# Stick-breaking scans and products in pieces of 512 keys, key blocks taken from the highest down

## The chip, the core and the metric

The kernel runs on one core of one Trainium2 chip. The metric is the device time of one execution in microseconds (us). Five engines work from queues of their own and in the order of these queues: PE (matrix products, with PEld for its weight loads), DVE (vector work), ACT (activation functions and copies), POOL (GpSimd, elementwise work here) and SP, which issues nearly all DMAs.

## What is computed

One decoder layer: RMSNorm, one input projection, 8 heads of forgetting attention (softmax with a decay), 8 heads of stick-breaking attention, output projection, RMSNorm, a gated MLP with a causal convolution, final norm. 1024 positions, model width 1024, head width 64, float32. The change lies in the stick-breaking heads:

```
z = einsum('bhqd,bhkd->bhqk', q, k) * scale          # 128 queries, all keys
mask = kpos < qpos
log_one_minus = where(mask, log_sigmoid(-z), 0)
after = reverse cumsum over keys of log_one_minus, the key itself left out
weights = where(mask, exp(log_sigmoid(z) + after), 0)
out = weights @ v
```

So the weight of key s is sigmoid(z[s]) times the product of (1 - sigmoid(z[j])) over the keys j that lie between s and the query. The kernel works with the product itself: a running product from the last key down to the first.

## The kernel before

All matrix work is in float32r with operands split into a high and a low part, so that most products are three matmuls (`mm3`, lines 159 to 161) or, with the low half of one side left out, two.

**Attention** runs over 16 heads, the forgetting heads first (`p < NFOX`), then the 8 stick-breaking heads. A head has 8 query blocks `i` of 128, of which block i sees n = (i + 1) * 128 keys. Blocks 2g and 2g + 1 form group g, and the groups are taken in the order 0, 1, 3, 2 (`ORDER`).

`score(p, hb, i, ws)` (line 449) handles one query block: PE writes scores into PSUM in chunks of up to 512 keys (lines 466 to 470), ACT writes sigmoid(-z) into a tile `qt` and sigmoid(z) into `w[i]` (lines 480, 481). Two `qt` tiles (`NQ`) take turns; in traces they have the name `fbt`. Then, for a stick-breaking head, DVE makes the running product over all n columns of `qt` in place, from the highest column down (`tensor_tensor_scan`, line 493), and POOL multiplies `w` with it, shifted by one column (line 494). In the text this POOL operation is "the product".

`trans(g, mm, ws, box)` (line 497) transposes the weights of both blocks of a group for keys 256 mm to 256 mm + 255 on PE into a PSUM tile `tp` of 128x512 (line 505; there are two such tiles), ACT copies it into the high half `ph` (line 513), and DVE subtracts for the low half `pl` (line 514). A `tp` tile is free once `pl` is done. The tile on the diagonal (mm = g) needs three transposes in place of four and has tiles of its own, `pth` and `ptl`, 384 wide; the full ones share two pairs `ph`, `pl`.

`pv(p, hb, g, mm, box)` (line 517) multiplies V with the tile: four matmuls of 256 columns, two with the high half (line 525) and two with the low half (line 526), all of them summed in the one PSUM tile `o`. After the last, DVE folds `o` into the output (lines 534, 535).

**What sets the order.** `attention_stream` (line 566) writes the work of attention as a list: the scores of both blocks of a group, then the transposes and V products of the group before it (`prev`), three transposes ahead of the first V product (`LAG`). So the transposes of group 1 come behind the scores of blocks 6 and 7, those of group 3 behind the scores of blocks 4 and 5, and those of group 2 behind the first two blocks of the next head. Between the pieces `fill_to` puts matmuls of other work (projections of later heads, later the output projection), by costs that are written into the list. From this program order a scheduler sets the queues of PE, DVE, ACT and POOL; SP's queue stays as written.

POOL has other work in its queue as well: splitting weights (`wh`, `wl`, lines 142, 143), the low half of the projected q and k (`hl`, line 237) and sums (`oacc`, line 554).

Of the kernel before, what the change touches and what calls it, by code (L numbers as in the profile page):

```python
# [13 lines left out]
ALU = mybir.AluOpType  # L14
# [5 lines left out]
T = 1024  # L20
# [3 lines left out]
NFOX = 4  # L24
# [44 lines left out]
def layer(ctx, tc, xT, wqk, wv0, wv, wout, wup, wdn, cols, fbias, yT):  # L69
# [379 lines left out]
    def score(p, hb, i, ws):  # L449
        fox = p < NFOX  # L450
        q, kh, kl, vt, fbt = heads[p, hb]
        n = (i + 1) * P
        w = pp.tile([P, T], F32, name="w")
        ws[i] = w
        m = None
        if not fox:
            if len(qi) < NQ:
                qi.append(fp.tile([P, T + 1], F32, name="fbt"))
                nc.gpsimd.memset(qi[-1][:, T:T + 1], 1.0)
            qt = qi[count[0] % NQ]  # L460
            count[0] += 1
        for c0, cn in CHUNKS[i]:
            s = ps_s.tile([P, 512], F32, name="s")
            qb = q[:, i * P:(i + 1) * P]
            diag = c0 <= i * P < c0 + cn
            nc.tensor.matmul(s[:, :cn], qb, kh[:, c0:c0 + cn], start=True, stop=False)
            nc.tensor.matmul(s[:, :cn], qb, kl[:, c0:c0 + cn], start=False, stop=not diag)
            if diag:
                o = i * P - c0
                nc.tensor.matmul(s[:, o:o + P], identb, mask_f if fox else mask_s,  # L470
                                 start=False, stop=True)
            un = min(cn, n - c0)
            if fox:
                m2 = small.tile([P, 1], F32, name="m")
                nc.vector.tensor_tensor_reduce(  # L475
                    out=w[:, c0:c0 + un], in0=s[:, :un], in1=fbt[:, c0:c0 + un], scale=-1.0,
                    scalar=3.0e38 if m is None else m, op0=ALU.add, op1=ALU.min, accum_out=m2)
                m = m2
            else:
                act(qt[:, T - n + c0:T - n + c0 + un], s[:, :un], AF.Sigmoid, scale=-1.0)  # L480
                act(w[:, c0:c0 + un], s[:, :un], AF.Sigmoid)

        if fox:
            l = small.tile([P, 1], F32, name="l")
            act(w[:, :n], w[:, :n], AF.Exp, scale=-1.0, bias=m, accum_out=l)  # L485

            def rest():
                nc.vector.reciprocal(l, l)  # L488
                nc.gpsimd.tensor_scalar(w[:, :n], w[:, :n], l, 1.0, ALU.mult, ALU.mult)  # L489
        else:  # L490
            def rest():
                rev = slice(T - 1, T - n - 1 if n < T else None, -1)
                nc.vector.tensor_tensor_scan(qt[:, rev], qt[:, rev], qt[:, rev], 1.0, ALU.mult, ALU.bypass)  # L493
                nc.gpsimd.tensor_tensor(w[:, :n], w[:, :n], qt[:, T - n + 1:T + 1], ALU.mult)  # L494
        defer(0, rest)

    def trans(g, mm, ws, box):
# [18 lines left out]

    def pv(p, hb, g, mm, box):
        vt = heads[p, hb][3]
        if mm == 0:
            box["o"] = ps_o.tile([P, 256], F32, name="o")  # L520
        o = box["o"]
        ph, pl = box[mm]
        for a, kb in enumerate((2 * mm + 1, 2 * mm)):
            sl = slice(a * 256, (a + 1) * 256)
            nc.tensor.matmul(o, vt[:, kb, :], ph[:, sl], start=(mm == 0 and a == 0), stop=False)  # L525
            nc.tensor.matmul(o, vt[:, kb, :], pl[:, sl], start=False, stop=(mm == g and a == 1))  # L526
        if mm == g:
            h0 = hb * 64
            r, r2 = slice(h0, h0 + 64), slice(64 - h0, 128 - h0)
            ot = heads["o", p]  # L530
# [35 lines left out]
    def attention_stream():  # L566
# [3 lines left out]
        for n, (p, hb) in enumerate(hs):  # L570
            ws = {}
            order = ORDER_LAST if n == len(hs) - 1 else ORDER
            for gi, g in enumerate(order):
# [5 lines left out]
                    yield cost, partial(score, p, hb, i, ws)  # L579
                yield from prev  # L580
                box = {}
                tr = [(TRC, partial(trans, g, mm, ws, box)) for mm in range(g + 1)]
                pvs = [(0.67 - TRC, partial(pv, p, hb, g, mm, box)) for mm in range(g + 1)]
                prev = tr[:LAG]
                for mm in range(g + 1):
                    prev.append(pvs[mm])
# [708 lines left out]
```

## Time and profile before

| | |
|---|---|
| Median of 3 runs | 1442.48 us (1440.78 to 1443.48) |
| Profiled execution: its own time | 1441.58 us |
| Profiled execution: span of the core | 1439.6 us |
| PE busy | 1317.6 us, 92% |
| DVE, POOL, ACT busy | 1116.7, 859.4, 620.8 us (78%, 60%, 43%) |
| Stick-breaking heads | about 345 to 645 us of the span |

The span is what the trace covers; the execution's own time is 2 us longer. An engine that waits for a semaphore is not busy, but one that has started an instruction and is held up inside it is: a long instruction in the trace may be a held one. Matmuls are pipelined and their durations overlap, so that four matmuls of 0.28 us that start 0.12 us apart take 0.6 us. In a timeline, a number in brackets behind a row is the time that the engine stood idle before it, with the instruction that ended the wait.

### The profile page before, as it was taken

Reading aid. Unit: us, or ns where it says so; the run is one execution under the profiler, and the core shown is the slowest. Engines: PE = TensorE matmul, PEld = TensorE weight load, DVE = VectorE, ACT = ScalarE, POOL = GpSimd, SP = SyncE. Lnnn points to the kernel's source line nnn. Section 1 sums busy time; section 2 is a strip of 40 time slices with the busy share of each in tenths; the row PEclk is TensorE's granted clock in tenths of the full one; section 3 lists DMA queues with packets and bytes.
Section 4 is the critical chain, followed back from the end, with each engine's and each line's share of the span. In section 5 each row is a group of like instructions: output and inputs, shape, how many; then the busy total and the mean of one; then the engine's idle time right before and its main releaser. Section 6 shows DMA issues by size and latency. Waiting matters only on the chain.

```text
span 1439.6 us, 19147 instructions
## 1 busy us (share of the span) xinstructions
PE 1317.6 (92%) x6640; PEld 1075.9 (75%) x6640; DVE 1116.7 (78%) x1588; ACT 620.8 (43%) x1128; POOL 859.4 (60%) x730
## 2 busy tenths in 40 slices
PE   7899999999898887889778899999999998999995
PEld 5878878877787765777556688888888865878785
DVE  6246555655676677786899999998888889899987
ACT  5134434444454554353443434443443354344334
POOL 7344454543747573455667788878878763454423
PEclk9999999999999999999889999999999998999997
DMA  5556555545444454547311233333322355554313
GB/s 179 183 161 187 152 154 163 147 147 135 149 121 124 119 159 143 179 147 270 125 44 59 84 106 110 110 110 110 110 97 95 96 176 204 180 171 132 126 36 117
DMA packets 97232, 194.89 MB, mean 135 GB/s; under 512 B 8680, under 2 KB 35688, under 8 KB 97136
## 3 DMA queue, kind: packets, MB, share of 16 engines
q1 hardware_dynamic: 96272, 193.04, 42.6%
q8 instruction: 52, 0.85, 0.3%
q10 hardware_dynamic: 864, 0.64, 0.1%
q14 instruction: 44, 0.36, 0.1%
HBM read 132.79 MB, written 60.85 MB: 135 GB/s over the span
## 4 chain that ended last, share of the span: by engine, by line
PE 50%; DMA 18%; DVE 16%; POOL 7%; issue 6%; SPq 2%; ACT 2%; DVEq 0%; POOLq 0%; ACTq 0%
PE u L161 8%; PE u L160 8%; PE u L159 8%; PE pj L159 5%; PE pj L161 5%; PE pj L160 5%; DMA q<-qkd 4%; DVE fbt L493 3%; DMA vd<-vs 3%; DMA wraw<-in_wqk_dram 2%; DMA wraw<-in_wv_dram 2%; PE tp L505 2%; DMA fbt<-nfd 2%; PE o L526 2%; PE o L525 1%
## 5 line engine op out<-in xcount | busy, mean ns | idle before, releaser
L143 POOL TENSOR_TENSOR wl<-wraw,wh 128x256 fp32r<-128x256 f32 (+2 forms) x134 | 125.3, 952 | 26.9 <-ACT wh L140 21.3
L494 POOL TENSOR_TENSOR w<-w,fbt 128x128 f32<-128x128 f32 (+3 forms) x64 | 90.1, 1417 | 84.4 <-DVE fbt L493 59.9
L904 ACT CAST wh<-s 128x512 fp32r<-128x512 f32 (+1 forms) x136 | 79.8, 591 | 125.7 <-POOL s L879 71.0
L493 DVE TENSOR_TENSOR_SCAN fbt<-fbt 128x128 f32<-128x128 f32 (+3 forms) x64 | 103.5, 1624 | 25.9 <-ACT fbt L480 22.0
L142 POOL TENSOR_SCALAR wh<-wraw 128x256 fp32r<-128x256 f32 (+1 forms) x112 | 55.3, 509 | 108.8 <-DMA wraw<-in_wqk_dram 60.7
L878 POOL TENSOR_TENSOR s<-wraw 128x512 f32<-128x512 f32 (+1 forms) x34 | 55.8, 1641 | 96.0 <-DVE wl L906 53.5
L505 PE MATMUL tp<-ident,w 128*128 128x128 f32 x576 | 94.0, 281 | 19.5 <-DVE pl L514 9.5
L159 PE MATMUL pj<-xh,wh 128*128 128x512 f32 x224 | 103.1, 460 | 5.1 <-DVE yf L293 5.1
L906 POOL TENSOR_TENSOR wl<-wraw,wh 128x512 fp32r<-128x512 f32 x60 | 102.9, 1722 | 0.6 <-ACT wh L904 0.6
L505 PEld LDWEIGHTS tp<-ident,w 128*128 128x128 f32 x576 | 70.7, 144 | 39.1 <-DVE pl L514 12.6
L906 POOL TENSOR_TENSOR wl<-s,wh 128x512 fp32r<-128x512 f32 x48 | 88.5, 1845 | 13.8 <-ACT wh L904 13.4
L514 DVE TENSOR_TENSOR pl<-tp,ph 128x512 fp32r<-128x512 f32 x96 | 64.9, 685 | 40.9 <-ACT ph L513 40.5
L161 PE MATMUL pj<-xh,wl 128*128 128x512 f32 x224 | 91.9, 410 | 0.0
L160 PE MATMUL pj<-xl,wh 128*128 128x512 f32 x224 | 91.3, 407 | 0.0
L485 ACT ACTIVATE w<-w,m 128x128 f32<-128x128 f32 (+3 forms) x64 | 49.7, 776 | 91.1 <-DVE m L475 86.0
L1003 DVE SCALAR_TENSOR_TENSOR tg<-ua,col,tg 128x1023 f32<-128x1023 f32 (+1 forms) x44 | 88.1, 2002 | 0.0
L480 ACT ACTIVATE fbt<-s 128x512 f32<-128x512 f32 (+2 forms) x96 | 47.8, 498 | 83.8 <-PE s L470 39.2
L489 POOL TENSOR_SCALAR w<-w,l 128x128 f32<-128x128 f32 (+3 forms) x64 | 47.6, 748 | 59.9 <-DVE l L488 32.7
L904 ACT CAST wh<-wraw 128x512 fp32r<-128x512 f32 (+1 forms) x96 | 55.1, 589 | 63.1 <-DMA wraw<-in_wdn_dram 25.0
L1003 DVE SCALAR_TENSOR_TENSOR tv<-ub,col,tv 128x1023 f32<-128x1023 f32 (+1 forms) x44 | 76.0, 1727 | 5.7 <-ACT tv L1001 5.6
L513 ACT CAST ph<-tp 128x512 fp32r<-128x512 f32 x96 | 55.7, 590 | 53.1 <-PE o L525 33.4
L885 POOL TENSOR_TENSOR s<-wraw 128x512 f32<-128x512 f32 (+1 forms) x34 | 56.4, 1658 | 35.7 <-DVE wl L906 33.4
(409 smaller groups left out, 4569.4 us busy)
## 6 DMA issues: line engine op xcount, KB each, us to landing
wraw<-in_wup_dram SPq DMA_DIRECT2D x47, 512.0 KB, 3.6
qkd<-hl SPq DMA_DIRECT2D x32, 512.0 KB, 2.9
td<-tg SPq DMA_DIRECT2D x44, 256.0 KB, 2.3
vd<-vs SPq DMA_DIRECT2D x32, 256.0 KB, 4.5
q<-qkd SPq DMA_DIRECT2D x16, 512.0 KB
kh<-qkd SPq DMA_DIRECT2D x32, 256.0 KB, 16.6
kl<-qkd SPq DMA_DIRECT2D x32, 256.0 KB, 17.4
vt<-vd SPq DMA_DIRECT2D x16, 512.0 KB, 17.9
```

Source lines behind the costliest of these rows:

```text
L143: nc.gpsimd.tensor_tensor(self.lo[:, sl], self.raw[:, sl], f32(self.hi[:, sl]), ALU.subtract)
L159: nc.tensor.matmul(ps, ah, bh, start=start, stop=False)
L160: nc.tensor.matmul(ps, ah, bl, start=False, stop=False)
L161: nc.tensor.matmul(ps, al, bh, start=False, stop=stop)
L493: nc.vector.tensor_tensor_scan(qt[:, rev], qt[:, rev], qt[:, rev], 1.0, ALU.mult, ALU.bypass)
L494: nc.gpsimd.tensor_tensor(w[:, :n], w[:, :n], qt[:, T - n + 1:T + 1], ALU.mult)
L505: nc.tensor.transpose(tp[:, a * 256 + b * P:a * 256 + (b + 1) * P], ws[2 * g + b][:, kb * P:(kb + 1) * P], ident)
L514: nc.vector.tensor_tensor(pl[:, z:], tp[:, z:], f32(ph[:, z:]), ALU.subtract)
L885: nc.gpsimd.tensor_tensor(d["s3"], g[:, :w], v[:, :w], ALU.subtract)
L904: nc.scalar.copy(h[:, o:o + w], src)
L906: eng.tensor_tensor(l[:, o:o + w], src, f32(h[:, o:o + w]), ALU.subtract)
L1003: nc.vector.scalar_tensor_tensor(t[:, s:], us[:, :T - s], col[:, cw + tap:cw + tap + 1], t[:, s:], op0=ALU.mult, op1=ALU.add)
```

## The change

In stick-breaking heads the scan and the product are cut at key 512. For n up to 512 there is one of each as before. For n = 640, 768, 896 and 1024 the upper piece (128, 256, 384 or 512 columns) is scanned first, starting from 1.0, and then the lower piece of 512, starting from the last value of the upper one, which it reads from `qt`. Each piece has its own product; as the product is shifted by one column, the pieces there are n - 511 and 511 wide.

Transposes and V products of a stick-breaking head take the key pairs from mm = g down to 0 in place of 0 up to g, so that the diagonal tile comes first. The forgetting heads stay as they were.

```
-                rev = slice(T - 1, T - n - 1 if n < T else None, -1)
-                nc.vector.tensor_tensor_scan(qt[:, rev], qt[:, rev], qt[:, rev], 1.0, ALU.mult, ALU.bypass)
-                nc.gpsimd.tensor_tensor(w[:, :n], w[:, :n], qt[:, T - n + 1:T + 1], ALU.mult)
+                z = T - n
+                for a in range((n - 1) // 512 * 512, -1, -512):
+                    b = min(n, a + 512)
+                    rev = slice(z + b - 1, z + a - 1 if z + a else None, -1)
+                    nc.vector.tensor_tensor_scan(qt[:, rev], qt[:, rev], qt[:, rev],
+                                                 1.0 if b == n else qt[:, z + b:z + b + 1],
+                                                 ALU.mult, ALU.bypass)
+                    b = n if b == n else b - 1
+                    sl = slice(a - 1 if a else 0, b)
+                    nc.gpsimd.tensor_tensor(w[:, sl], w[:, sl], qt[:, z + sl.start + 1:z + sl.stop + 1],
+                                            ALU.mult)
...
-        if mm == 0:
+        begin, end = (0, g) if p < NFOX else (g, 0)
+        if mm == begin:
             box["o"] = ps_o.tile([P, 256], F32, name="o")
...
-            nc.tensor.matmul(o, vt[:, kb, :], ph[:, sl], start=(mm == 0 and a == 0), stop=False)
-            nc.tensor.matmul(o, vt[:, kb, :], pl[:, sl], start=False, stop=(mm == g and a == 1))
-        if mm == g:
+            nc.tensor.matmul(o, vt[:, kb, :], ph[:, sl], start=(mm == begin and a == 0), stop=False)
+            nc.tensor.matmul(o, vt[:, kb, :], pl[:, sl], start=False, stop=(mm == end and a == 1))
+        if mm == end:
...
-                tr = [(TRC, partial(trans, g, mm, ws, box)) for mm in range(g + 1)]
-                pvs = [(0.67 - TRC, partial(pv, p, hb, g, mm, box)) for mm in range(g + 1)]
+                keys = range(g + 1) if p < NFOX else range(g, -1, -1)
+                tr = [(TRC, partial(trans, g, mm, ws, box)) for mm in keys]
+                pvs = [(0.67 - TRC, partial(pv, p, hb, g, mm, box)) for mm in keys]
```

Line numbers of the changed kernel are a few higher: 493, 494 become 496 and 501, the low half 514 becomes 522, V products 525 and 526 become 534 and 535.

DVE's queue in the third stick-breaking head, from the scans of blocks 6 and 7 to the `pl` subtractions of group 3 (`fbt` is the scan tile, `full` belongs to a projection), before:

```order
L493 SCALAR_TENSOR_TENSOR fbt<-fbt 128x896
L493 SCALAR_TENSOR_TENSOR fbt<-fbt 128x1024
L514 TENSOR_TENSOR pl<-tp,ph 128x512
L514 TENSOR_TENSOR ptl_577<-tp,pth_576 128x384
L534 COPY tm<-o 64x256
L535 TENSOR_TENSOR ot<-o,tm 64x256
L493 SCALAR_TENSOR_TENSOR fbt<-fbt 128x640
L232 SCALAR_TENSOR_TENSOR full<-pj,rbc 128x512
L493 SCALAR_TENSOR_TENSOR fbt<-fbt 128x768
L514 TENSOR_TENSOR pl<-tp,ph 128x512 x3
L514 TENSOR_TENSOR ptl_575<-tp,pth_574 128x384
```

and now:

```order
L496 SCALAR_TENSOR_TENSOR fbt<-fbt 128x384
L496 SCALAR_TENSOR_TENSOR fbt<-fbt 128x512 x3
L522 TENSOR_TENSOR ptl_577<-tp,pth_576 128x384
L522 TENSOR_TENSOR pl<-tp,ph 128x512
L543 COPY tm<-o 64x256
L544 TENSOR_TENSOR ot<-o,tm 64x256
L496 SCALAR_TENSOR_TENSOR fbt<-fbt 128x128
L496 SCALAR_TENSOR_TENSOR fbt<-fbt 128x512
L232 SCALAR_TENSOR_TENSOR full<-pj,rbc 128x512
L496 SCALAR_TENSOR_TENSOR fbt<-fbt 128x256
L522 TENSOR_TENSOR ptl_575<-tp,pth_574 128x384
L496 SCALAR_TENSOR_TENSOR fbt<-fbt 128x512
```

At the first place four scans of 384, 512, 512 and 512 stand where there were two, still in one piece ahead of group 1's low halves (now `ptl`, then `pl`). At the second the diagonal `ptl` of group 3 stands ahead of the last scan piece (512), and the `pl` follow behind it; in six of the eight heads all four pieces are ahead of `ptl`.

PE's queue in the second stick-breaking head, the end of group 3's V products and the scores of the next head's first block (`pj` is filling work), before:

```order
L525 MATMUL o<-ph,vt 128x256
L526 MATMUL o<-pl,vt 128x256
L525 MATMUL o<-pth_574,vt 128x256
L526 MATMUL o<-ptl_575,vt 128x256
L525 MATMUL o<-pth_574,vt 128x256
L526 MATMUL o<-ptl_575,vt 128x256
L466 MATMUL s<-kh,q 128x256
L467 MATMUL s<-kl,q 128x256
L470 LDWEIGHTS identb
L470 MATMUL s<-mask_s,identb 128x128
```

and now:

```order
L534 MATMUL o<-ph,vt 128x256
L535 MATMUL o<-pl,vt 128x256
L466 MATMUL s<-kh,q 128x256
L534 MATMUL o<-ph,vt 128x256
L467 MATMUL s<-kl,q 128x256
L470 LDWEIGHTS identb
L470 MATMUL s<-mask_s,identb 128x128
L277 MATMUL pj<-wh,xh_236 128x256
L278 MATMUL pj<-wl,xh_236 128x256
L279 MATMUL pj<-wh,xl_244 128x256
L277 MATMUL pj<-wh,xh_237 128x256
L535 MATMUL o<-pl,vt 128x256
```

The diagonal tile (`pth`, `ptl`) was the last of the four V products and has gone to the front, so it is not in these rows any more. The last is now a full tile, and the next head's scores and filling matmuls stand between its first and second matmul.

## Rows read from the trace of the kernel before

**Rows 1.** The page, part 1: busy us (share of the span) xinstructions.
```profile
PE 1317.6 (92%) x6640; PEld 1075.9 (75%) x6640; DVE 1116.7 (78%) x1588; ACT 620.8 (43%) x1128; POOL 859.4 (60%) x730
```

**Rows 2.** Busy time by stretch, the stick-breaking heads; the columns in the first row.
```profile
core 0: us, PE busy (x) PEld busy (x) DVE busy (x) ACT busy (x) POOL busy (x), PEclk, DMA share, GB/s
...
345.00:645.00 300.00, 258.96 (x1520) 214.78 (x1519) 218.65 (x280) 148.48 (x314) 175.22 (x165) 0.95 0.47 141
...
```

**Rows 3.** Waits, 345 to 645: waiting <- awaited: us in total, times, longest.
```profile
POOL w L494 <- DVE fbt L493: 59.9, 21, 8.6
...
ACT ph L513 <- PE o L525: 21.3, 6, 8.6
ACT fbt L480 <- POOL w L494: 19.5, 8, 6.9
...
PE o L526 <- DVE pl L514: 10.8, 5, 3.2
...
PE tp L505 <- DVE pl L514: 6.1, 5, 2.0
...
PE tp L505 <- POOL w L494: 5.4, 4, 3.6
```

**Rows 4.** Timeline, second head, DVE then POOL: start, us, instruction [idle before <- releaser].
```profile
402.07 2.02 DVE L493 TENSOR_TENSOR_SCAN fbt<-fbt 128x896 f32<-128x896 f32 x1
405.02 3.17 DVE L493 TENSOR_TENSOR_SCAN fbt<-fbt 128x1024 f32<-128x1024 f32 x1 [0.92 <-ACT fbt L480]
...
408.75 0.68 DVE L514 TENSOR_TENSOR pl<-tp,ph 128x512 fp32r<-128x512 f32 x1
...
404.26 1.77 POOL L494 TENSOR_TENSOR w<-w,fbt 128x896 f32<-128x896 f32 x1 [3.11 <-DVE fbt L493]
408.36 2.00 POOL L494 TENSOR_TENSOR w<-w,fbt 128x1024 f32<-128x1024 f32 x1 [2.32 <-DVE fbt L493]
```

**Rows 5.** Timeline, third head, DVE then POOL, and POOL in the last head.
```profile
437.86 5.60 DVE L493 TENSOR_TENSOR_SCAN fbt<-fbt 128x896 f32<-128x896 f32 x2 [1.87 <-ACT fbt L480]
443.38 0.66 DVE L514 TENSOR_TENSOR pl<-tp,ph 128x512 fp32r<-128x512 f32 x1
...
438.31 3.00 POOL L237 TENSOR_TENSOR hl<-full,hl 128x512 fp32r<-128x512 f32 x1
441.27 5.71 POOL L494 TENSOR_TENSOR w<-w,fbt 128x896 f32<-128x896 f32 x2
...
618.16 3.00 POOL L143 TENSOR_TENSOR wl<-wraw,wh 128x512 fp32r<-128x512 f32 x1
```

**Rows 6.** Timeline of PE: four of its waits, and two matmuls in a row.
```profile
409.48 0.39 PE L526 MATMUL o<-pl,vt 128*128 128x256 f32 x1 [1.79 <-DVE pl L514]
409.70 0.28 PE L525 MATMUL o<-ph,vt 128*128 128x256 f32 x1
409.82 0.29 PE L526 MATMUL o<-pl,vt 128*128 128x256 f32 x1
...
444.10 0.39 PE L526 MATMUL o<-pl,vt 128*128 128x256 f32 x1 [2.20 <-DVE pl L514]
...
452.12 0.66 PE L505 MATMUL tp<-ident,w 128*128 128x128 f32 x4 [1.05 <-DVE pl L514]
...
480.10 0.39 PE L526 MATMUL o<-pl,vt 128*128 128x256 f32 x1 [3.21 <-DVE pl L514]
```

**Rows 7.** Timelines: scans of 512 and 1024 and a product of 512 alone.
```profile
574.66 1.22 DVE L493 TENSOR_TENSOR_SCAN fbt<-fbt 128x512 f32<-128x512 f32 x1
...
544.36 2.28 DVE L493 TENSOR_TENSOR_SCAN fbt<-fbt 128x1024 f32<-128x1024 f32 x1
...
400.06 1.09 POOL L494 TENSOR_TENSOR w<-w,fbt 128x512 f32<-128x512 f32 x1 [1.25 <-PE s L467]
```

**Rows 8.** Timelines of ACT and DVE: copy and subtraction of a full tile.
```profile
419.28 0.59 ACT L513 CAST ph<-tp 128x512 fp32r<-128x512 f32 x1 [1.53 <-PE o L525]
...
419.90 0.69 DVE L514 TENSOR_TENSOR pl<-tp,ph 128x512 fp32r<-128x512 f32 x1 [1.33 <-ACT ph L513]
```

## The prediction

> **What bounds the kernel now.** The first view is the page's busy table: PE is busy for 1317.6 of 1439.6 us, 92%, DVE for 78% and POOL for 60% [rows 1]. So the reader should look for the places where PE, in spite of that, stands still, and only those in which the changed lines run. The changed lines run in the second half of attention, from 345 to 645 us. The table by stretch gives PE 258.96 busy of 300 us there [rows 2], so about 41 us are idle. The table of waits of the same stretch says on what [rows 3]: V products wait 10.8 us for the low halves `pl` (DVE), transposes wait 6.1 us for the same `pl`, because the two PSUM tiles `tp` are freed by it, and transposes wait only 5.4 us for a finished product (POOL). The longest wait of the list, POOL 59.9 us for scans, is POOL being idle and costs nothing by itself.
>
> The timeline then shows why `pl` is late. At **place A**, V products of key pair group 1, `pl` stands on DVE behind the scans of query blocks 6 and 7: scan of 896 at 402.07, scan of 1024 from 405.02 for 3.17 us, `pl` at 408.75 [rows 4], and PE has waited 1.79 us [rows 6]. The same place costs 2.20 and 3.21 us in the next two heads [rows 6]. At **place B**, third transposes of group 3, `pl` stands behind the scans of blocks 4 and 5 (1.05 us in one head) [rows 6].
>
> What decides the length of these scans is POOL. A scan of 1024 takes 2.28 us when it is alone [rows 7], but 3.17 us where the product of 896 (404.26, 1.77 us) was already running: 406.03 is its end, and 406.03 plus 2.28 is 408.31, the scan's end within 0.1 us [rows 4]. So the scan did not share, it stood until the product was done. The reverse stands in rows 5: a POOL subtraction came at 438.31, inside a scan, and took 3.00 us, and two scans that need 2.02 and 2.28 us alone took 5.60 us together. The queue is scan (to 439.9), subtraction (to 441.3, so some 1.3 us), scan, and only then both products (5.71 us for 1.77 and 2.00 us of work) [rows 4, 5, 7]. A POOL operation that is waiting gets in at the boundary between two scans, and then DVE's turn comes. `pl` itself, which reads PSUM, runs at its usual length beside a product of 2.00 us [rows 4].
>
> The Trainium skill, page "SBUF — State Buffer", section "Who interferes with whom", states the same as a rule: a DVE instruction with two SBUF inputs and a GpSimd instruction that reads SBUF exclude one another for the whole instruction, and the one that issues first has it. By that rule a scan cut in two offers POOL one entry more in the middle, which speaks against this change; without it the products would simply run under the next scan. The trace agrees with the rule (3.17 us against 2.28 us alone).
>
> **The change, part by part.**
>
> Fixed costs. Blocks 4 to 7 of 8 heads get two scans and two products in place of one: 32 more of each. Two scans of 512 take 2 x 1.22, one of 1024 takes 2.28 us: 0.16 us per cut, 5.1 us of DVE in all. Two products of 512 take 2 x 1.09 against 2.00 us: 0.18 per cut, 5.8 us of POOL [rows 4, 7]. Neither engine is the bound, so this counts only at places A and B. The slope is (2.28 - 1.22)/512, 2.1 ns a column, and (2.00 - 1.09)/512, 1.8 ns, for products; so by estimate scans of 384, 256 and 128 take 0.96, 0.69 and 0.43 us, of 640 and 768 1.49 and 1.75 us, products of 384 and 128 0.87 and 0.41, of 640 1.32 us. The lower scan now starts from a value that the upper one wrote and waits for it; behind it on DVE stand the `pl` subtractions and the folds, for which PE waits.
>
> Place A. The order on DVE shows that nothing overtakes: where scans of 896 and 1024 stood ahead of `pl`, now 384, 512, 512, 512 do. Before, back to back: scan 2.02, product 1.77, scan 2.28, in all 6.07 us. After: POOL hears of the finished upper scan about 0.17 us later (404.09 to 404.26 [rows 4]), so the lower scan goes first; from then on they alternate: 0.96 + 1.22 + 0.87 + 1.22 + 1.09 + 1.22, 6.58 us. That is **+0.5 us**. Where another POOL operation was queued ahead of the products, as in rows 5, the line before was scan, subtraction, scan: 2.02 + 1.3 + 2.28, 5.6 us, with both products after `pl`. Now it is 0.96 + 1.3 + 1.22 + 0.87 + 1.22 + 1.09 + 1.22, 7.9 us: **+2.3 us**. I count three heads of that kind (the first, the third, the last; the last head's is the POOL subtraction at 618.16 [rows 5]) and five of the first: 9.4 us. PE's 10.8 us at this place are 5 waits [rows 3], so three heads (one of 2.3, two of 0.5) have no wait there that a delay would lengthen in full, and I take half of their 3.3: **7.8 us**. The bounds: 0.3 us for two fixed costs in the five heads that wait (1.6 us), and 2.3 us in all eight (18 us). A gain is excluded only as far as the alternation holds: if POOL never got in, the four scans would take 4.6 us and each place would gain about 1 us. I take the alternation, since rows 5 show it directly.
>
> Place B. The same arithmetic: 1.49 + 1.32 + 1.75 (scan and product of 640, scan of 768), 4.56 us before; 0.43 + 1.22 + 0.41 + 0.69 + 1.09 + 1.22, 5.06 us after: +0.5 us. Against it the first tile is now the diagonal one, whose `pl` is 384 wide instead of 512, a quarter of 0.69 us [rows 8] less, 0.15 us or so. In two heads (third and last) the new DVE order puts that diagonal `pl` ahead of the last scan piece, which helps the third transposes but delays the fourth, since the second `pl` comes after the piece: I put these at nothing. Six heads at 0.35 us: **2 us**, bounds -6.1 (all of the waits in rows 3 gone) and 4.
>
> Place C, new. In group 3 there are three full tiles and one diagonal one, and only two `ph`/`pl` pairs for the full ones. Before, the third full tile waited on the first V product, with a transpose and filling matmuls behind it (ACT waits such as 1.53 us in rows 8 hurt nobody). Now the diagonal one comes first and the last full tile waits on the V product two places ahead: copy 0.59, `pl` 0.69 [rows 8], about 1.4 us with the signals, against 4 matmuls at 0.12 us [rows 6] and the next head's scores that the order moved in between (0.5 to 1 us). Remainder 0.2 us in 8 heads: **1.6 us**, bounds 0 and 4.
>
> Gains of earlier products: PE waits for products only 5.4 us, 4 times [rows 3], nearly all of it where blocks of 256 to 512 keys are concerned, which are not cut. ACT waits 19.5 us for products that free the scan tile [rows 3], but with the alternation the last piece ends no earlier. Nothing.
>
> Sum: 7.8 + 2 + 1.6, 11.4 us on PE's path. I take off a quarter, as a wait made longer at A also lets POOL and DVE catch up before B: **+8 us**. The profiled execution took 1441.58 us (span 1439.6), so 1449.6; it lies 0.9 us under the median of 1442.48. On the median: 1450.5. I predict 1450.
>
> **The rivals.**
> Faster: the diagonal tiles come first and need only the upper piece, so PE's 6.1 us of waiting at B go and the products' 5.4 us shrink. For it: in two heads the diagonal `pl` does overtake a scan piece. Against it: in six it doesn't, and at B PE waits for DVE, not for POOL. It decides where POOL doesn't get in at the new boundary. Price -3 to -8 us: 1434 to 1439.5. Chance 0.13.
> No change: the alternation is real, but the waits at A are taken from slack, since scans often stand for ACT anyway (the scan of 1024 in rows 4 began 0.92 us after the one of 896 had ended). Then only fixed costs stay, 8 heads by 0.3 us: 1441 to 1445, in the middle 1444. Chance 0.20.
> Much slower: POOL gets in at every boundary of every head, so all eight heads pay 2.3 us at A, and PE's longer pauses cost clock (in this stretch the granted clock was 0.95 on the mean [rows 2]): 1456 to 1462. Chance 0.12.
>
> **How the numbers follow.** Forecast (1445.5 to 1456) 0.55, faster 0.13, no change 0.20, much slower 0.12. A measurement here tells about 0.2%, 2.9 us, from no change. So slower 0.67, same 0.20, faster 0.13. The range leaves out most of the faster case and the end of the much slower one: 1440 to 1459.
>
> **What would show it.** In the profile after: 96 scans with pieces of 512 that take 1.2 us alone and 2.1 to 2.3 us where a product was running; V products that wait for `pl` and `ptl` together more than the 10.8 us, by 5 to 10; transposes that wait for `pl` about as long as before; a new wait of the last V product of group 3 for ACT or DVE, 0.1 to 0.5 us each; PE busy unchanged in the sum, DVE and POOL busy up by at least 5 us each. The prediction is wrong if scans of 512 ahead of `pl` follow each other without a product between them, or if the waits at A shrink.

## The result, and the profile after

The changed kernel takes 1459.88 us (median of 4 runs, 1456.54 to 1462.12), the kernel before on the same chip 1441.63 us (1440.77 to 1443.48): ratio 1.0123, 95% interval 1.0099 to 1.0146. On two other chips the ratio is 1.0096 (1.0075 to 1.0118) and 1.0118 (1.0098 to 1.0138). So it is slower by 14 to 18 us. The forecast was 1450, with 1459 as the end of the range: the sign was right, and the 8 us too small for the 18 on that chip.

The profiled execution took 1460.76 us (span 1459.0). First the page's busy table, then the busy time of the stick-breaking stretch, which now ends at 664 us in place of 645 (columns as in [rows 2]):

```profile
PE 1324.8 (91%) x6640; PEld 1083.5 (74%) x6640; DVE 1126.2 (77%) x1620; ACT 622.9 (43%) x1128; POOL 875.6 (60%) x762
```

```profile
345.00:664.00 319.00, 266.46 (x1526) 222.31 (x1525) 231.32 (x313) 150.29 (x315) 193.46 (x197) 0.93 0.46 135
```

The span is 19.4 us longer, and about 19 us of that lie in this stretch. PE idles 319 - 266.46, 52.5 us, against 41.0 in [rows 2]: 11.5 us more. The other 7.5 us are PE being busy longer with the same work (266.46 against 258.96), while the mean granted clock of the stretch goes from 0.95 to 0.93. DVE has its 32 more instructions and 9.5 us more, POOL 32 more and 16.2 us more [rows 1].

The waits of the same stretch (waiting <- awaited: us in total, times, longest):

```profile
POOL w L501 <- DVE fbt L496: 53.0, 30, 4.6
...
PE o L535 <- DVE ptl L522: 19.4, 13, 3.7
...
PE tp L513 <- DVE ptl L522: 10.9, 7, 3.4
...
PE tp L513 <- POOL w L501: 6.6, 1, 6.6
```

The diagonal tile comes first, so PE now waits for its `ptl` where it waited for `pl`. Transposes wait 10.9 us for a DVE half where they waited 6.1, and for products 6.6 in one wait (in the first head) where there were 5.4 [rows 3]. DVE halves that the V products and transposes wait for, `pl` and `ptl` together: 20.0 us for V products (14.7 before, of that 3.9 for `ptl`) and 11.6 for transposes (6.1).

The timeline of the second head, DVE then POOL, and then the third head, shows the new boundary:

```profile
408.75 2.28 DVE L496 TENSOR_TENSOR_SCAN fbt<-fbt 128x384 f32<-128x384 f32 x2
411.70 3.43 DVE L496 TENSOR_TENSOR_SCAN fbt<-fbt 128x512 f32<-128x512 f32 x2 [0.67 <-ACT fbt L480]
...
415.70 0.55 DVE L522 TENSOR_TENSOR ptl<-tp,pth 128x384 fp32r<-128x384 f32 x1
...
409.88 2.85 POOL L501 TENSOR_TENSOR w<-w,fbt 128x385 f32<-128x385 f32 x2 [2.04 <-DVE fbt L496]
413.99 3.08 POOL L501 TENSOR_TENSOR w<-w,fbt 128x513 f32<-128x513 f32 x2 [1.25 <-DVE fbt L496]
```

```profile
445.07 7.18 DVE L496 TENSOR_TENSOR_SCAN fbt<-fbt 128x384 f32<-128x384 f32 x4 [1.87 <-ACT fbt L480]
452.17 0.53 DVE L522 TENSOR_TENSOR ptl<-tp,pth 128x384 fp32r<-128x384 f32 x1
...
445.53 1.93 POOL L237 TENSOR_TENSOR hl<-full,hl 128x512 fp32r<-128x512 f32 x1
447.43 6.76 POOL L501 TENSOR_TENSOR w<-w,fbt 128x385 f32<-128x385 f32 x4
```

In the third head two scans stood together before and took 5.60 us, while the subtraction `hl` was held for 3.00 us [rows 5]. Now four pieces, which need 0.96 + 3 x 1.22 = 4.6 us alone [rows 7 for the 512], take 7.18 us: DVE lost 2.6 us, because `hl` gets in after the first piece and a product piece after each of the next two. `hl` is the winner (1.93 us), the DVE half behind the scans the loser. PE's rows at this place (place A, heads two and three) and two of the longest at the third transposes (place B):

```profile
416.30 0.38 PE L535 MATMUL o<-ptl,vt 128*128 128x256 f32 x1 [1.92 <-DVE ptl L522]
...
452.75 0.55 PE L535 MATMUL o<-ptl,vt 128*128 128x256 f32 x1 [3.68 <-DVE ptl L522]
...
535.20 0.69 PE L513 MATMUL tp<-ident,w 128*128 128x128 f32 x2 [3.36 <-DVE ptl L522]
...
613.16 1.08 PE L513 MATMUL tp<-ident,w 128*128 128x128 f32 x4 [3.28 <-DVE ptl L522]
```

The second head's wait hardly grew (1.79 before), the third's grew by 1.5 (2.20 before) [rows 6].

### The profile page after: what moved, and what is told of

Same layout as the page of the kernel before. It is cut to its first block, busy times and chain, and to the rows that moved or that the text cites. A ratio compares the mean times of both kernels' runs of the same rounds, so it can differ in the third digit from the quotient of the medians.

```text
span 1459.0 us, 19213 instructions
## 1 busy us (share of the span) xinstructions
PE 1324.8 (91%) x6640; PEld 1083.5 (74%) x6640; DVE 1126.2 (77%) x1620; ACT 622.9 (43%) x1128; POOL 875.6 (60%) x762
## 4 chain that ended last, share of the span: by engine, by line
PE 52%; DMA 18%; DVE 15%; POOL 6%; issue 5%; SPq 2%; ACT 2%; DVEq 0%; ACTq 0%; POOLq 0%
PE u L160 9%; PE u L161 9%; PE u L159 9%; PE pj L159 5%; PE pj L161 5%; PE pj L160 5%; DMA q<-qkd 5%; DVE fbt L496 4%; DMA vd<-vs 3%; DMA kl<-qkd 2%; PE tp L513 2%; PE o L535 2%; DMA wraw<-in_wqk_dram 2%; PE o L534 2%; DMA fbt<-nfd 1%
## 5 line engine op out<-in xcount | busy, mean ns | idle before, releaser
L501 POOL TENSOR_TENSOR w<-w,fbt 128x128 f32<-128x128 f32 (+6 forms) x96 | 113.2, 1194 | 78.8 <-DVE fbt L496 53.0
L143 POOL TENSOR_TENSOR wl<-wraw,wh 128x256 fp32r<-128x256 f32 (+2 forms) x134 | 124.5, 946 | 23.4 <-ACT wh L140 19.4
L496 DVE TENSOR_TENSOR_SCAN fbt<-fbt 128x128 f32<-128x128 f32 (+3 forms) x96 | 112.6, 1180 | 27.2 <-ACT fbt L480 24.6
L513 PE MATMUL tp<-ident,w 128*128 128x128 f32 x576 | 94.3, 282 | 25.6 <-DVE ptl L522 10.9
L888 POOL TENSOR_TENSOR s<-wraw 128x512 f32<-128x512 f32 (+1 forms) x34 | 55.7, 1637 | 93.7 <-DVE wl L916 50.4
L522 DVE TENSOR_TENSOR pl<-tp,ph 128x512 fp32r<-128x512 f32 x96 | 65.2, 685 | 45.2 <-ACT ph L521 44.7
L916 POOL TENSOR_TENSOR wl<-s,wh 128x512 fp32r<-128x512 f32 x48 | 87.8, 1831 | 14.7 <-ACT wh L914 14.4
L480 ACT ACTIVATE fbt<-s 128x512 f32<-128x512 f32 (+3 forms) x96 | 47.6, 495 | 92.3 <-PE s L470 37.7
L277 PE MATMUL pj<-wh,xh 128*128 128x256 f32 (+1 forms) x256 | 78.6, 307 | 1.0 <-DVE yf L293 1.0
```

Source lines behind the costliest of these rows:

```text
L143: nc.gpsimd.tensor_tensor(self.lo[:, sl], self.raw[:, sl], f32(self.hi[:, sl]), ALU.subtract)
L277: nc.tensor.matmul(ps[:, :n], xh[k][:, sl], h, start=(k == 0), stop=False)
L501: nc.gpsimd.tensor_tensor(w[:, sl], w[:, sl], qt[:, z + sl.start + 1:z + sl.stop + 1], ALU.mult)
L513: nc.tensor.transpose(tp[:, a * 256 + b * P:a * 256 + (b + 1) * P], ws[2 * g + b][:, kb * P:(kb + 1) * P], ident)
L522: nc.vector.tensor_tensor(pl[:, z:], tp[:, z:], f32(ph[:, z:]), ALU.subtract)
L916: eng.tensor_tensor(l[:, o:o + w], src, f32(h[:, o:o + w]), ALU.subtract)
```

## The experiments

Each kernel below was timed beside the kernel before on the same chip, whose median there was 1445.9 to 1446.7 us. Microseconds in the table are the ratio's distance from 1 times 1446.

| Kernel | Ratio (95% interval) | us against before |
|---|---|---|
| scans and products cut, keys ascending, three chips | 1.0077 (1.0056 to 1.0097), 1.0076 (1.0053 to 1.0100), 1.0080 (1.0055 to 1.0104) | +11, +11, +12 |
| keys descending, nothing cut | 1.0001 (0.9989 to 1.0012) | 0 |
| scans cut, products whole, two chips | 1.0066 (1.0048 to 1.0084), 1.0061 (1.0038 to 1.0083) | +10, +9 |
| products cut, scans whole | 0.9995 (0.9983 to 1.0008) | -1 |
| before, second operand of the scans in PSUM | 0.9937 (0.9914 to 0.9961) | -9 |
| changed kernel, the same | 0.9940 (0.9920 to 0.9959) | -9 |
| cut, keys ascending, the same | 0.9947 (0.9930 to 0.9965) | -8 |
| scans in pieces of 256, products whole | 1.0077 (1.0050 to 1.0104) | +11 |
| scans of 896 and 1024 cut alone | 1.0032 (1.0016 to 1.0048) | +5 |
| scans of 640 and 768 cut alone | 1.0005 (0.9990 to 1.0020) | +1 |
| changed kernel, two chips | 1.0096 (1.0075 to 1.0118), 1.0118 (1.0098 to 1.0138) | +14, +17 |
| scans cut, products whole, keys descending | 1.0096 (1.0062 to 1.0130) | +14 |

### Which part of the change costs the time

My theory was that the price stands at the new scan boundary, where POOL gets in. The rivals were the order of the key blocks, and the fixed cost of more instructions. First each part alone. The cut alone is the kernel before with the new `rest()` of the diff, and the order alone is the changed kernel with the old `rest()`.

> The cut of scans and products alone, key blocks of transposes and V products ascending as before. Theory 1 (the price is the cut: at each new scan boundary a product piece of POOL gets in before the next scan, which makes the DVE operation that PE waits for later, at eight third-transpose places and eight V-product places, and PE's clock falls in the longer gaps): 1452 to 1459 us, PE waits at the third transposes like those of the changed kernel, about 3 us a head, and granted clock in the stick-breaking stretch about 0.93. Theory 2 (the price is the descending order, which makes the diagonal pair's transposes and its split first and so waits for the highest block's product): within 4 us of the kernel before, 1441 to 1446 us.

> The descending key order alone, scans and products whole. Theory 1: 1441 to 1446 us, of that about 2 us in the first head, where the diagonal's transpose now waits for the product of block 3. Theory 2: 1452 to 1460 us, with PE waits for the transposed diagonal pair in every head.

The cut alone costs 11 us, on three chips; the order alone costs nothing. So the cut is the cause of most of it. The expected place was wrong. With ascending keys, 345 to 655 us:

```profile
PE o L534 <- DVE pl L522: 17.1, 7, 3.8
...
PE tp L513 <- DVE pl L522: 5.4, 5, 2.7
```

The V products wait 17.1 us for `pl` (10.8 before) and the transposes 5.4 (6.1 before), so here nearly all of the rise in waits for DVE halves is at the V products.

Then the two halves of the cut:

```
-                nc.vector.tensor_tensor_scan(qt[:, rev], qt[:, rev], qt[:, rev], 1.0, ALU.mult, ALU.bypass)
+                for a in range((n - 1) // 512 * 512, -1, -512):
+                    b = min(n, a + 512)
+                    rev = slice(z + b - 1, z + a - 1 if z + a else None, -1)
+                    nc.vector.tensor_tensor_scan(qt[:, rev], qt[:, rev], qt[:, rev],
+                                                 1.0 if b == n else qt[:, z + b:z + b + 1],
+                                                 ALU.mult, ALU.bypass)
```

with the product as it was, and the other way round, with the scan as it was:

```
-                nc.gpsimd.tensor_tensor(w[:, :n], w[:, :n], qt[:, T - n + 1:T + 1], ALU.mult)
+                for a in range((n - 1) // 512 * 512, -1, -512):
+                    b = min(n, a + 512)
+                    b = n if b == n else b - 1
+                    sl = slice(a - 1 if a else 0, b)
+                    nc.gpsimd.tensor_tensor(w[:, sl], w[:, sl], qt[:, z + sl.start + 1:z + sl.stop + 1], ALU.mult)
```

> The scans cut in two, the products whole, key blocks ascending. Theory 1 (a boundary costs only where a piece of product is ready to get in at it; here a block's product waits for both of its scan pieces, so only the product of the block before can): 1443 to 1450 us, PE waits at the third transposes less than half of those of the changed kernel. Theory 3 (the fixed cost of 32 more scans and the slower clock that follows is enough): 1450 us or more, near the changed kernel's time.

> The products cut in two (upper piece first), the scans whole, key blocks ascending. Theory 1 (DVE's scan and POOL's product shut each other out for a whole instruction): at the V products of the second group the scan of 1024 waits for half a product (0.9 us) and not a whole one (1.8 us) and the split behind it comes 0.9 us earlier, in 8 heads 7 us at most, less what the product pieces lose to it later: 1435 to 1443 us. Theory 3 (fixed cost): 1444 to 1450 us, from 32 more POOL operations of about 0.15 us each and the splits they hold up.

The scan cut alone costs 9 us, the product cut alone nothing. By the times expected, both results spoke for theory 3, the fixed cost (1450 us or more for the scan cut, 1444 to 1450 for the product cut; measured 1456.97 and 1445.58), and only the runs below decide against it. I had expected the scan cut to be the cheaper of the two, on the idea that with whole products little is ready at the new boundary. The timeline of its third head, DVE then POOL, shows that something is:

```profile
448.93 7.24 DVE L496 TENSOR_TENSOR_SCAN fbt<-fbt 128x384 f32<-128x384 f32 x4 [1.87 <-ACT fbt L480]
456.09 0.66 DVE L519 TENSOR_TENSOR pl<-tp,ph 128x512 fp32r<-128x512 f32 x1
...
449.38 1.94 POOL L237 TENSOR_TENSOR hl<-full,hl 128x512 fp32r<-128x512 f32 x1
452.57 2.51 POOL L499 TENSOR_TENSOR w<-w,fbt 128x896 f32<-128x896 f32 x1 [1.25 <-DVE fbt L496]
```

The four pieces take 7.24 us again. Before, three POOL operations stood at this place and one of them got in, at the one boundary between the two scans [rows 5]. With three boundaries two of them do, `hl` and the whole product of 896 (held itself: 2.51 for 1.77 us of work [rows 4]). A boundary lets in whatever POOL has next; it needn't be a piece of the product.

The product cut was a miss of my theory: I expected up to 7 us of gain, since a scan would wait for half a product only. In its trace the V products' wait for `pl` does fall (10.8 to 8.2 us), but the transposes wait longer for products (5.4 to 8.3), and the time stays.

### Whether it is the exclusion

The scan has two SBUF inputs, both of them `qt`; the second is ignored by the bypass. If the exclusion hangs on that second input, it can be taken away without touching any order: let the ignored operand be a column of PSUM. A zero column beside the V products' accumulator serves.

```
+    oz = ps_o.tile([P, 512], F32, name="oz")
+    nc.vector.memset(oz[:, 256:257], 0.0)
+    zero = oz[:, 256:257]
...
-                nc.vector.tensor_tensor_scan(qt[:, rev], qt[:, rev], qt[:, rev], 1.0, ALU.mult, ALU.bypass)
+                nc.vector.tensor_tensor_scan(qt[:, rev], qt[:, rev], zero.to_broadcast([P, n]), 1.0, ALU.mult, ALU.bypass)
...
-            box["o"] = ps_o.tile([P, 256], F32, name="o")
+            box["o"] = oz[:, :256]
```

> The kernel before, whole scans and products, but the scan's second operand, which the bypass ignores, is one zero column of PSUM instead of the SBUF row itself. Theory 1 (a scan with two SBUF inputs and a POOL operation shut each other out for a whole instruction): with one SBUF input left the two run side by side, the pair of scans at the V products of the third head's second group takes 4.3 us instead of 5.6, that of the second head's 1024 block 2.3 instead of 3.2, and the splits behind them come as much earlier: 8 to 14 us below the kernel before. Theory 3 (fixed costs of instructions only, and no exclusion that depends on the operands): within 3 us of the kernel before, or slower by what a PSUM operand costs a scan.

> The changed kernel with the same zero column of PSUM as the scans' second operand. Theory 1: no POOL operation gets in at a boundary any more, what is left of the cut is its fixed cost of about 0.2 us per boundary: from 8 us below the kernel before to 4 us above it, at least 10 us below the changed kernel. Theory 3: 11 to 19 us above the kernel before, as the changed kernel.

> Scans and products cut in two, key blocks ascending, and the scans' second operand a zero column of PSUM. Without exclusion the cut has only its fixed cost, beside work that PE doesn't wait for: 6 to 11 us below the kernel before, as with whole scans. If finer pieces bring the splits and transposes forward once nothing gets in between, 12 us or more below it; if the fixed cost of 32 boundaries (0.2 us each on DVE) counts, 1 to 5 us below it.

All three run 8 to 9 us below the kernel before, and so beat both kernels: medians 1437.06, 1437.13 and 1438.68 us. With the second SBUF operand gone, the change as a whole costs nothing any more, neither the cut nor the order. So its 14 to 18 us need that operand, as the exclusion says. The third head of the kernel before with this one edit, DVE then POOL:

```profile
433.37 4.20 DVE L496 TENSOR_TENSOR_SCAN fbt<-fbt,oz 128x896 f32<-128x896 f32 x2 [1.05 <-ACT fbt L483]
437.49 0.67 DVE L517 TENSOR_TENSOR pl<-tp,ph 128x512 fp32r<-128x512 f32 x1
...
433.45 1.29 POOL L237 TENSOR_TENSOR hl<-full,hl 128x512 fp32r<-128x512 f32 x1
435.56 1.77 POOL L497 TENSOR_TENSOR w<-w,fbt 128x896 f32<-128x896 f32 x1 [0.81 <-DVE fbt L496]
```

The two scans take 4.20 us (5.60 before), and `hl` (1.29, before 3.00) and the product of 896 (1.77) run under them. Over all eight heads, the scans of 1024 (out<-in xcount | busy us, mean ns of one | idle before), first in the kernel before and then with the PSUM operand:

```profile
L493 DVE TENSOR_TENSOR_SCAN fbt<-fbt 128x1024 f32<-128x1024 f32 x8 | 23.5, 2941 | 1.0 <-ACT fbt L480 0.9
```

```profile
L496 DVE TENSOR_TENSOR_SCAN fbt<-fbt,oz 128x1024 f32<-128x1024 f32 x8 | 18.2, 2273 | 0.9 <-ACT fbt L483 0.8
```

The mean of 1024 is now 2.27 us, which is the scan alone [rows 7]. So what a scan took beyond that came with the second SBUF operand, beside POOL's work. PE's waits for `pl` follow, 345 to 645 us, but there is a new wait, the first row:

```profile
PE oz L528 <- DVE fbt L496: 4.3, 5, 1.6
...
PE tp L508 <- DVE pl L517: 1.9, 4, 0.9
...
PE oz L529 <- DVE pl L517: 0.8, 2, 0.7
```

Of 10.8 us of V products and 6.1 of transposes [rows 3], 0.8 and 1.9 are left. The new wait is a price of this edit: the zero column lies in the tile `oz` into which the V products are summed, and now their first matmul waits for scans that read it. With the cut it is longer, 6.4 us with keys descending and 9.2 ascending. No V product ran during any of these scans.

The Trainium skill, page "SBUF — State Buffer", section "Who interferes with whom", states that a DVE instruction with at most one SBUF input (outside its two-port modes) doesn't contend with GpSimd. These scans agree: 2.27 us on the mean beside running products.

The same operand in the changed kernel shows the fixed cost of the cut by itself. In its third head the four pieces take

```profile
433.55 4.69 DVE L499 TENSOR_TENSOR_SCAN fbt<-fbt,oz 128x384 f32<-128x384 f32 x4 [1.05 <-ACT fbt L483]
```

4.69 us against 4.20 for two whole scans: 0.25 us per cut on DVE, where the prediction had 0.16. The three kernels take the same time, so this cost stands beside other work. The third theory, fixed costs, was tested from the other side too, with pieces of 256 (two or three boundaries per block where there was one):

```
+                step = n if n <= 512 else 256
+                for a in range((n - 1) // step * step, -1, -step):
+                    b = min(n, a + step)
...
```

The product stays whole here.

> Scans of blocks above 512 keys in pieces of 256, products whole, key blocks ascending: three boundaries more for each 1024 or 896 block's two, ten per pair of blocks at two places where the version with pieces of 512 has four. Theory 3 (each boundary has its price on DVE, some 0.2 us): 10 us for pieces of 512 become 20 to 32 us above the kernel before. Theory 1 with exclusion alone (what a boundary costs is the POOL operation that it lets in, and there are no more whole products or other POOL operations ready than at pieces of 512): 10 to 16 us above it.

48 scans more than with pieces of 512, and 11 us against 9: no difference that these intervals can tell, where I expected 20 us or more of fixed costs alone. It fits the exclusion, if there are only so many POOL operations to let in; how many got in was not counted. (One reservation: in this kernel's third head one of the pieces stands behind `pl`, so the DVE order isn't quite the same.)

### Where in a head the price arises

The next two cut scans only at place A (blocks of 896 and 1024 keys) and only at place B (640 and 768), with products whole and keys ascending, by `step = 512 if n > 768 else n` and `step = 512 if 512 < n <= 768 else n`.

> Scans cut in two only for the blocks of 896 and 1024 keys, which stand ahead of the second group's V products (place A); products whole, key blocks ascending. By the prediction's sizes (7.8 of 11.4 us at A) this is 7 to 10 us above the kernel before, nearly all of what cutting every scan costs (10 us). By the rise of the waits in the changed kernel's trace, more at the third group's transposes (5.5 us) than at A (3.5 us), it is 3 to 5 us.

> Scans cut in two only for the blocks of 640 and 768 keys, which stand ahead of the third group's transposes (place B); products whole, key blocks ascending. By the prediction's sizes 1 to 3 us above the kernel before; by the rise of the waits in the changed kernel's trace 4 to 7 us.

Cut at A alone the kernel loses 5 us (2 to 7), less than the 7 to 10 by the prediction's sizes; at B alone 1 (-1 to 3), at both 9. The waits of the first, 345 to 650 us, tell more than the time:

```profile
PE o L532 <- DVE pl L520: 20.5, 8, 3.8
...
PE tp L511 <- POOL w L500: 5.5, 4, 3.7
...
PE tp L511 <- DVE pl L520: 3.2, 4, 1.5
```

V products wait 20.5 us for `pl`, 9.7 more than before. But PE's idle time of the stretch (305 - 259.77 = 45.2 us) is only 4.2 us longer, since the transposes wait 2.9 us less for `pl` and other waits shrink too. So it seems that what PE loses at A, DVE and POOL in part use to catch up. With every scan cut that is gone; the waits of the scan cut, 345 to 660 us:

```profile
PE o L531 <- DVE pl L519: 18.4, 8, 3.8
...
PE tp L510 <- POOL w L499: 6.8, 4, 5.1
PE tp L510 <- DVE pl L519: 6.5, 6, 2.8
```

V products wait 7.6 us more, and transposes at B 6.5, as much as before: the lengthened scans at B use up the lead. That 9 is more than 5 + 1 is at the edge of what the intervals resolve (3.9 us, give or take 3.7); the rows make the reason plausible, and I count it as shown only so far.

### What the order adds

With the cut, the descending order isn't free. One chip ran the changed kernel, the cut alone, and the scan cut with and without the descending order.

> The changed kernel itself, on the chip on which the other versions run. If the order of the key blocks costs only together with the cut, 15 to 19 us above the kernel before, against 11 for the cut alone; if the two do not add, 10 to 13 us above.

> The changed kernel beside the cut alone on one chip. If the descending order adds to the cut: 3 to 6 us above the cut alone, with waits at the seventh head's transposes of the third group that the ascending order doesn't have. If it adds nothing and the chips differed: within 2 us of the cut alone.

> The cut of scans and products with key blocks ascending once more, beside the others on their chip. If the descending order adds nothing to the cut, 11 to 17 us above the kernel before, as the changed kernel; if it adds some 3 to 6 us, 8 to 11 us above it.

> The cut of scans and products, key blocks ascending: 10 to 12 us above the kernel before, as on two other chips.

> Scans cut, products whole, key blocks ascending: 8 to 11 us above the kernel before, as on another chip.

> Scans cut, products whole, key blocks descending. If the order adds to any scan cut: 3 to 6 us above the same with ascending blocks. If it adds nothing: within 2 us of it.

With +14 for the changed kernel on one chip and +11 for the cut alone on another the question was open. On the common chip the changed kernel stands 5.5 us above the cut alone (1.0118 against 1.0080), the scan cut with descending keys 5.1 us above the one with ascending keys; taken together 5.3 us, give or take 3.6. In three profiles of the changed kernel the transposes wait 11.6 to 11.9 us for DVE halves, in three of the cut alone 5.4 to 5.9, while the V products wait about as long in both. One place can be read. The seventh head on the common chip, DVE then POOL, first the changed kernel, then the cut alone:

```profile
606.61 2.07 DVE L496 TENSOR_TENSOR_SCAN fbt<-fbt 128x256 f32<-128x256 f32 x2
608.60 2.56 DVE L663 TENSOR_TENSOR t<-xin,t 128x512 f32<-128x512 f32 x2
611.09 0.55 DVE L522 TENSOR_TENSOR ptl<-tp,pth 128x384 fp32r<-128x384 f32 x1
...
607.46 3.15 POOL L501 TENSOR_TENSOR w<-w,fbt 128x257 f32<-128x257 f32 x2 [3.84 <-DVE fbt L496]
```

```profile
607.80 0.68 DVE L522 TENSOR_TENSOR pl<-tp,ph 128x512 fp32r<-128x512 f32 x1
608.44 1.29 DVE L661 TENSOR_TENSOR t<-xin,t 128x512 f32<-128x512 f32 x2
```

and PE, two rows of the changed kernel, then one of the cut alone:

```profile
606.75 0.51 PE L159 MATMUL pj<-ogh,wh 128*128 128x512 f32 x1 [2.84 <-DVE t L662]
...
611.69 0.84 PE L513 MATMUL tp<-ident,w 128*128 128x128 f32 x4 [3.27 <-DVE ptl L522]
```

```profile
607.94 0.79 PE L159 MATMUL pj<-ogh,wh 128*128 128x512 f32 x1 [4.32 <-DVE t L660]
```

In the changed kernel the `ptl` for which the third transposes wait (3.27 us there) stands behind two additions of the output projection, which also have two SBUF inputs and are held by the products: 2.56 us for 1.29. With ascending keys, where `pl` stands ahead of them, the transposes don't wait here; the projection matmul before them waits 1.5 us longer instead, so the two waits together are 6.1 us against 4.3. The scan cut with whole products and descending keys has no such wait of the transposes either, at 6.3 us of transposes waiting for `ptl`. Its profiled execution, 1471.61 us, was the slowest of six (the others took 1452 to 1459), with PE busy for 1333.1 us, so its rows are a poor guide to its 5 us. The lengths of the heads, from one head's first score matmul to the next one's, point the same way in both pairs: the seventh takes 3.9 to 4.1 us longer than in the kernel before in three profiles of the changed kernel and -1.2 to 1.3 in three of the cut alone; with products whole it is 3.1 with keys descending, and 1.0 and -0.8 ascending. So the size of the order's share is measured, give or take 3.6, and its place only in part.

## Why the prediction was wrong, step by step

**Bound and mechanism: right.** That scans and POOL operations stand for each other, that POOL gets in at the new boundary, and that the halves behind the scans make PE wait, is what the timelines and the PSUM operand showed: without the second SBUF operand the change costs nothing. In the third head four pieces were worked out at 7.9 us and took 7.18; in the second 6.58 us were worked out from the first scan to the last, and it was 415.13 - 408.75 = 6.4.

**The first step that failed: the quarter taken off.** The sum was 11.4 us, and PE's idle time in the stretch rose by 11.5, in two further profiles of the changed kernel by 14.3 and 12.0 (315 - 259.70 = 55.3 and 319 - 265.93 = 53.1 us, against 41.0). I took a quarter off, since a longer wait at A would let DVE and POOL catch up before B. The cut at A alone speaks for such a catching up (9.7 us more waiting of V products, 2.9 less of transposes, 4.6 us of time). But the change cuts at B as well, and there the transposes' waits don't shrink: 11.6 us in place of 6.1. The same text that gave B longer scans let B absorb A's delay. This step is worth 3 of the 10 us that were missing on that chip.

**The second step that failed: PE busy unchanged.** I put a loss of clock into the rival "much slower" alone, at 0.12, and at nothing in the sum. In the profiled execution PE was busy 7.2 us longer, which is most of the rest. In two further profiles of the changed kernel it was busy 1316.6 and 1320.7 us, where the one profile of the kernel before has 1317.6. So it is a term between -1 and 7 us that changes from one execution to the next. The forecast needed it with both ends, and the range would then have gone beyond 1459. Most of the difference between the three executions lies in the first head, where PE is busy for 38.0, 34.4 and 35.1 us with the same queue. In all three it first stands for a product, for 6.6, 6.2 and 4.7 us; behind that wait the granted clock, the third number from the end, is not the same. From 375 to 395 us, first the kernel before, then the profiled execution of the changed kernel, then its two further profiles:

```profile
375.00:395.00 20.00, 20.00 (x166) 19.65 (x167) 14.87 (x29) 12.13 (x26) 11.81 (x14) 0.99 0.34 119
```

```profile
375.00:395.00 20.00, 18.10 (x113) 17.54 (x112) 12.38 (x24) 9.80 (x20) 9.93 (x8) 0.74 0.27 92
```

```profile
375.00:395.00 20.00, 19.95 (x154) 19.47 (x155) 13.82 (x28) 11.73 (x25) 10.87 (x13) 0.92 0.35 115
```

```profile
375.00:395.00 20.00, 18.39 (x145) 17.43 (x144) 16.24 (x29) 11.39 (x24) 13.15 (x13) 0.96 0.41 142
```

The 0.74 is a mean over both levels of the clock: a score matmul of 512 columns takes 0.63 us at 384 us, and 0.39 at the upper level, 2.4 GHz, at 379 us of the kernel before. Why one execution gets the clock back sooner than another stays open.

**The terms behind the 11.4: wrong sizes that cancel.** That the sum met the 11.5 is luck. At place A I had 7.8 us, from 2.3 in each of the first, third and last head. The place was right. The changed kernel's wait for the first half in the first and in the last head, and the last head's before (the first head had none):

```profile
377.04 0.39 PE L535 MATMUL o<-ptl,vt 128*128 128x256 f32 x1 [1.90 <-DVE ptl L522]
...
641.05 0.58 PE L535 MATMUL o<-ptl,vt 128*128 128x256 f32 x1 [2.50 <-DVE ptl L522]
```

```profile
624.68 0.38 PE L526 MATMUL o<-pl,vt 128*128 128x256 f32 x1 [1.04 <-DVE pl L514]
```

With the third head's (2.20 before, 3.68 now) these waits rose by 1.9, 1.5 and 1.5 us where I had 2.3 each; in the second head it was 0.1, and in the fourth and the seventh they fell. (In the sixth head `ptl` does overtake the last scan piece at place A, which I had taken as excluded; V products wait 0.9 us there.) All V products of the stretch together wait 5.3 us more for `ptl` and `pl` (20.0 in place of 14.7), in the two further profiles 7.2 and 6.5; with ascending cuts 6 to 10 us more for `pl`. Place B I had at 2 us, on the ground that the diagonal half is narrower; it came to 5.5 (11.6 in place of 6.1), in the two further profiles 5.6 and 5.9. Most of that are two places: the fifth head (3.36 us in place of 1.72), where DVE needs 6.5 us from the first scan piece to the last instead of 5.15, and the seventh (3.28 us, none before), where whole additions with two SBUF inputs stand ahead of the first half too, which I had missed. Place C, 1.6 us, doesn't show: no V product of the last pair waits there in the timeline. The first head's transposes wait for the product longer, 6.6 us in place of 4.4. I had put that at nothing; that the order makes it is not shown, as it is 5.8 us in the cut with ascending keys and 4.7 with the order alone.

**The rivals.** "Faster" was to win where POOL doesn't get in at the new boundary. That is what the PSUM operand does, and then whole scans are as fast as pieces: the pieces' earlier products bring no gain there, though with the new wait for scans 2 to 5 us longer this is no clean test of them. "No change" fell, as the waits at A and at B did grow. "Much slower" gave the right time, but not for its reasons: its first condition, every head paying 2.3 us at A, did not hold (the second head's wait grew by 0.13 us), and its second, a loss of clock, is large in one profile of three.

**Which checks held.** The page counts 96 scans. DVE and POOL busy up by at least 5 us: 9.5 and 16.2. V products waiting 5 to 10 us more: 5.3 against the 14.7 of both halves. A new wait of the last V product of group 3: none. Transposes waiting about as long: no, nearly twice. PE busy unchanged: no, in the profiled execution.

## What to carry to other kernels

Where two engines shut each other out for whole instructions, a cut on one of them is an offer to the other at the new boundary; count what the other has queued there, not only the pieces of the same job. Before cutting, look whether the exclusion can be taken away: an operand that the operation ignores can lie in another memory, and here that one edit was worth 9 us where the change lost 14 to 18, in spite of the 4.3 us that V products now wait for the scans. And a discount for "catching up later" holds only if the later place keeps its old work: check whether the change burdens it too.

## What the runs showed of the hardware that I had not expected

A scan whose second operand is ignored by a bypass is still held up beside POOL work like an operation with two SBUF inputs: with that operand in SBUF 1024 columns took 2.94 us on the mean, with one PSUM column repeated 2.27. What a scan costs while PE sums into the same PSUM tile the runs don't show, since the V products waited for the scans. And an engine that is held up inside an instruction counts as busy: with the PSUM operand DVE's busy time on the page fell from 1116.7 to 1099.9 us and POOL's from 859.4 to 835.3, with the same work.

```profile
PE 1312.7 (92%) x6640; PEld 1070.5 (75%) x6640; DVE 1099.9 (77%) x1589; ACT 619.8 (43%) x1128; POOL 835.3 (58%) x730
```
